# Tokens requested sooner and two memory units run between the steps of the first projection

## The chip, the cores and the metric

The kernel runs on one core of a Trainium2 chip. A core has a matrix engine (TensorE, PE in the profile; its weight loads are PEld), a vector engine (VectorE, DVE), a scalar engine (ScalarE, ACT), GpSimd (POOL) and SyncE (SP), which here issues nearly all DMAs. Each engine works through its own list of instructions in order and waits on semaphores of the others. The metric is the device time of one execution in microseconds (us), the median of several.

## The reference, cut to what matters

```python
mem_n = rmsnorm(mem, norm_mem)                       # 256 memory tokens, width 1024
for i in range(2):                                   # layer 0: mixer A, layer 1: mixer B
    h = rmsnorm(x, norm_mix[i])                      # 1024 tokens, width 1024
    mk, mv = split(mem_n @ w_mem_kv[i])              # 4 memory heads of 64
    q, k, v, qm = split(h @ w_in[i])                 # one combined projection
    y_tok = windowed_gqa(q, k, v, sink) if i == 0 else neighbourhood_attn(q, k, v, rpb)
    y_mem = memory_attn(qm, mk, mv)
    x = x + concat(y_tok, y_mem) @ w_out[i]
    h = rmsnorm(x, norm_ffn[i])
    g, u = split(h @ w_gate_up[i])
    x = x + (silu(g) * u) @ w_down[i]
return rmsnorm(x, norm_final)
```

All arrays are float32. The kernel writes each operand of a product as a high part and a low part (the rest) and multiplies hh, hl and lh, so each 128x128 block of weights costs three products.

## The kernel before, in words

Everything is held transposed: features on the 128 partitions (8 blocks k), tokens along the free dimension in two halves of 512 (index 0 and 1). A "unit" is 128 columns of a weight matrix, 512 KB; `load_w` fetches it, `hi` (L106, a cast on ACT) and `lo` (L109, a subtraction on DVE or POOL) split it. `steps` (L139) multiplies a unit with a half: 8 steps of three matmuls, 24 in all, into one PSUM bank.

The memory stage stands at the start (pool `mp`). It splits the memory tokens (mhl, L301), runs eight memory units (w_mem[l, u], matmuls "mm<-mhl,wm" of 128x256), scales each result (mt, L345), and splits it into keys (mkh, mkl) or transposes it (mvT, L352) into values (mv). In between it prepares the tokens for layer 0. The class Norm squares them (sq on ACT, L196), adds the squares pairwise on DVE (L219), sums over partitions on PE (st, L212), and turns that into a factor: nv on DVE (L232), nr on POOL (L233), a diagonal matrix diag on DVE (L235), spread by one product bc on PE (L247). Then each of the 8 blocks gives h (L267, DVE) and its parts hT (ACT L106, DVE L109). There are three such norms in the stage: the memory's, token half 0's, token half 1's.

`first_dense` ends the stage. It runs three units of the first projection ("wf") on half 0 (72 matmuls of 128x512 "mm<-hT,wf"), and between their steps asks for the squares of half 1 and its norm. It leaves the three results in PSUM, in the list `pre`. It is called again for layer 1, behind the down projection (X, L1327, and the residual adds x, L1291, on DVE). The layer's code then reads `pre` out (`z.put(0, ps)`: copies to QS, KH, vT on ACT, L106, L410 and L464, and the low parts on DVE) and runs the same three units on half 1 (`z.half(1)`, 72 more matmuls). Behind them come memory scores (S, L567), transposes of v (vtr, L427), softmax rows (p) and so on.

PSUM has eight banks in four pools: ps_mm (2), ps_s (2, tag S), ps_t (3, tag T) and ps_o (1, tag O). `mm_tile` counts its calls in `wide[1]`; while `wide[0]` is set, counts 3 and 4 modulo 5 go to an S bank, 0 to a T bank, and 1 and 2 to ps_mm. The layer's code clears `wide[0]`, so half 1 takes ps_mm only. st, mvT and vtr take T banks, bc the O bank; in the down projection X takes ps_mm and S banks, Y the T and O banks.

The text of the kernel sets only dependences and priorities: a scheduler decides the order on each engine when the kernel is built, so the order is shown below as it comes out. Names there carry buffer numbers: mm_791 is the 791st object.

Of the kernel before, what the change touches and what calls it, by code (L numbers as in the profile page):

```python
# [9 lines left out]
F32 = mybir.dt.float32  # L10
F32R = mybir.dt.float32r
AF = mybir.ActivationFunctionType
ALU = mybir.AluOpType
# [4 lines left out]
P = 128  # L18
D = 1024
S = 1024  # L20
NK = D // P
HS = 512
HD = 64
NH = 12
NKV = 4
NMH = 4
# [15 lines left out]
def trunk_kernel(ctx: ExitStack, tc: tile.TileContext, a: dict, out: bass.AP):  # L42
# [58 lines left out]
    def raw_tile(name):  # L101

        return phase[0].tile([P, D], F32, tag="raw", name=name, bufs=phase[2])

    def hi(dst, src):
        nc.scalar.copy(dst, src)  # L106

    def lo(dst, src, h, eng=None):
        (eng or nc.vector).tensor_tensor(dst, src, h.bitcast(F32), op=ALU.subtract)  # L109

    def load_w(src, tag="whl", bufs=3, eng=None, name="w", pool=wp, parts=1):
        raw = raw_tile(f"{name}_raw")
        nc.sync.dma_start(raw, src)
        w = pool.tile([P, 2, D], F32R, tag=tag, name=name, bufs=bufs)
        for i in range(parts):
            c = slice(i * D // parts, (i + 1) * D // parts)
            hi(w[:, 0, c], raw[:, c])
            pieces = 4 if eng is nc.gpsimd else 1
            for j in range(pieces):
                n = D // parts // pieces  # L120
                cj = slice(i * D // parts + j * n, i * D // parts + (j + 1) * n)
                lo(w[:, 1, cj], raw[:, cj], w[:, 0, cj], eng)
        return w
# [9 lines left out]
    def steps(ps, w, h, order=range(NK), n=HS, start=True, stop=True):  # L133

        order = list(order)
        for i, k in enumerate(order):
            terms = three(wk(w, k), (h[k][:, 0, :n], h[k][:, 1, :n]))
            for j, (l, r) in enumerate(terms):
                nc.tensor.matmul(  # L139
                    ps[:, :n], l, r, start=start and i == 0 and j == 0,  # L140
                    stop=stop and i == len(order) - 1 and j == 2,
                )
            yield

    def run(g):
        for _ in g:
            pass

    def run_some(g, n):
        for _ in range(n):  # L150
            next(g, None)

    def first_dense(layer, norm):

        pre = []
        src = a["w_in_a"] if layer == 0 else a["w_in_b"]
        todo = (norm.add(x[k][1]) for k in range(len(norm.xs), NK))
        parts = norm.split(layer, hT[1], 4)
        for n, u in enumerate(FIRST[layer]):
            w = load_w(src[u], eng=None if layer == 0 else nc.gpsimd, name="wf")  # L160
            wide[:] = True, 2 + n
            ps = mm_tile()
            for i, _ in enumerate(steps(ps, w, hT[0])):
                if next(todo, 0) is not None and len(norm.xs) == NK and (n or i > 3):
                    next(parts, None)
            pre.append((w, ps))
        run(parts)
        return pre

    def mm_tile(name="mm"):  # L170

        wide[1] += 1
        if wide[0] and wide[1] % 5 > 2:
            return ps_s.tile([P, HS], F32, tag="S", name=name)
        if wide[0] and wide[1] % 5 == 0:
            return ps_t.tile([P, HS], F32, tag="T", name=name)
        return ps_mm.tile([P, HS], F32, tag="mm", name=name)

    def dense(w, h, n=HS):
        ps = mm_tile()  # L180
        run(steps(ps, w, h, n=n))
        return ps
# [96 lines left out]
    with tc.tile_pool(name="mp", bufs=1, reuse_waits="tile") as mp:  # L279
        phase[:] = mp, 8, 5  # L280
        memt = mp.tile([P, NK, NM], F32, name="memt")
        warm = mp.tile([P, P], F32, name="warm")
        nc.scalar.activation(warm, ones, AF.Square)
        wm0 = raw_tile("wm0")
        nc.sync.dma_start(memt[:, :2], a["mem"][:, :2])
        nc.scalar.dma_start(wm0[:, :HS], a["w_mem"][0, 0][:, :HS])
        nc.sync.dma_start(gains, a["gains"])
        nc.sync.dma_start(memt[:, 2:4], a["mem"][:, 2:4])
        nc.scalar.dma_start(wm0[:, HS:], a["w_mem"][0, 0][:, HS:])
        nc.sync.dma_start(memt[:, 4:], a["mem"][:, 4:])  # L290
        w0 = wp.tile([P, 2, D], F32R, tag="whl", name="wm", bufs=3)
        hi(w0[:, 0, :HS], wm0[:, :HS])
        lo(w0[:, 1, :HS], wm0[:, :HS], w0[:, 0, :HS])
        ws = [w0]


        mh = []
        mhl = mp.tile([P, NK, 2, NM], F32R, name="mhl")
        for k in range(NK):
            t, g = mhl[:, k], gains[:, 4, k : k + 1]  # L300
            nc.scalar.activation(t[:, 0], memt[:, k], AF.Copy, scale=g)  # L301
            nc.vector.scalar_tensor_tensor(
                t[:, 1], memt[:, k], g, t[:, 0].bitcast(F32), op0=ALU.mult, op1=ALU.subtract
            )
            mh.append(t)
            if k == 1:
                hi(w0[:, 0, HS:], wm0[:, HS:])
                lo(w0[:, 1, HS:], wm0[:, HS:], w0[:, 0, HS:])
        ws.append(load_w(a["w_mem"][0, 1], name="wm"))
        nc.sync.dma_start(ident, a["ident"])  # L310

        def load_x(f, k):
            x[k][f] = mp.tile([P, HS], F32, tag=f"x{k}{f}", name=f"x0_{k}{f}")
            nc.sync.dma_start(x[k][f], a["x"][k][:, f * HS : (f + 1) * HS])

        mem_norm = Norm(NM)
        for k in range(NK):
            mem_norm.add(memt[:, k])
        scale = mp.tile([P, NM], F32, name="mscale")
        nc.scalar.copy(scale, mem_norm.scale())  # L320

        hT = [[None] * NK, [None] * NK]
        norms = [Norm(), Norm()]
        kept = []
        for i in range(8):
            l, u = divmod(i, 4)
            if u == 0:
                kh = mp.tile([P, 2, NM], F32R, name=f"mkh{l}", tag="mkh", bufs=2)
                kl = mp.tile([P, 2, NM], F32R, name=f"mkl{l}", tag="mkl", bufs=2)
                vm = mp.tile([P, 2, NMH, 2, HD], F32R, name=f"mv{l}", tag="mv", bufs=2)  # L330
                kept.append((kh, kl, vm))
            if i + 2 < 8:
                ws.append(load_w(a["w_mem"][(i + 2) // 4, (i + 2) % 4], name="wm"))
            if i == 0:
                nc.sync.dma_start(sink, a["sink"].to_broadcast([P, NH]))
                nc.vector.tensor_scalar(nsink, sink, -1.0, None, op0=ALU.mult)
            if i < 3:
                for k in ((0, 1, 2), (3, 4, 5), (6, 7))[i]:
                    load_x(0, k)
            elif i < 7:  # L340
                for k in (2 * i - 6, 2 * i - 5):
                    load_x(1, k)
            ps = dense(ws[i], mh, NM)
            t = temp("mt", NM)
            nc.vector.tensor_tensor(t, ps[:, :NM], scale, op=ALU.mult)  # L345
            if u < 2:
                hi(kh[:, u], t)
                lo(kl[:, u], t, kh[:, u])
            else:
                tr = ps_t.tile([P, HS], F32, tag="T", name="mvT")  # L350
                for b in range(2):
                    nc.tensor.transpose(tr[:, b * P : (b + 1) * P], t[:, b * P : (b + 1) * P], ident)  # L352
                src = tr[:, :NM].rearrange("p (b i d) -> p b i d", b=2, i=2)
                m = 2 * (u - 2)
                for b in range(2):
                    hi(vm[:, b, m : m + 2, 0], src[:, b])
                    lo(vm[:, b, m : m + 2, 1], src[:, b], vm[:, b, m : m + 2, 0])
            if i in (1, 2):
                for k in range(4 * i - 4, 4 * i):
                    norms[0].add(x[k][0])  # L360
            if i == 2:
                parts = norms[0].split(0, hT[0])
            if i > 2:
                run_some(parts, 2)
            if i in (5, 6):
                for k in range(4 * i - 20, 4 * i - 16):
                    norms[1].add(x[k][1])
        pre = first_dense(0, norms[1])
        for l, (kh, kl, vm) in enumerate(kept):
            nc.sync.dma_start(memk_d[l, 0], kh.rearrange("p m k -> p (m k)").bitcast(F32))  # L370
            nc.sync.dma_start(memk_d[l, 1], kl.rearrange("p m k -> p (m k)").bitcast(F32))
            nc.sync.dma_start(memv_d[l], vm.rearrange("p b m i d -> p (b m i d)").bitcast(F32))
# [1158 lines left out]
```

## Time and profile before

| | us |
|---|---|
| runs of before, median (lowest to highest of 3) | 2138.86 (2138.51 to 2140.3) |
| the profiled execution, its own time | 2140.07 |
| its span | 2138.3 |
| PE busy, share of the span | 2099.2, 98% |
| DVE, ACT, POOL busy | 1516.3, 1062.4, 575.6 |
| mean granted clock of PE | 0.995 of full |
| memory stage, from the first matmul to the first memory scores of layer 0 | 5.85 to 86.56 |
| first projection of layer 1, both halves | 1044.16 to 1080.56 |

Rows of the profile name line, engine, operation and "out<-in" tiles. In a timeline the first number is the start in us from the span's start, the second the length of a group of like instructions, "x26" their count, and the bracket the idle time of that engine just before with the instruction that ended it. In windows, PEclk is the clock that was granted to PE, 1.00 being full. The pipelined matmuls of a group overlap, so a group's length divided by its count is the pitch of one.

### The profile page before, as it was taken

The page shows a single profiled execution, that of the slowest core. Times are in us where ns is not written, and L with a number is a line of the kernel's source. Part 1 is how long each engine was busy: PE and PEld are TensorE (multiplying, and loading weights), DVE is VectorE, ACT ScalarE, POOL GpSimd, SP SyncE. Part 2 cuts the span into 40 slices and gives each one's busy share as a digit, 9 for nine tenths or more (in the row PEclk, how much of TensorE's full clock was granted, in tenths as well). Part 3 has the DMA queues.
Part 4 walks back from the last instruction along what each step waited for, and adds up shares of the span by engine and source line. Part 5 has one row for each costly group of instructions (what it writes and reads, how often), then busy time and mean ns, then how long its engine had stood idle before and what let it go on. Part 6 is the DMA issues. An engine that isn't in the chain of part 4 may idle for free.

```text
span 2138.3 us, 29072 instructions
## 1 busy us (share of the span) xinstructions
PE 2099.2 (98%) x10308; PEld 1753.4 (82%) x10308; DVE 1516.3 (71%) x2485; ACT 1062.4 (50%) x2042; POOL 575.6 (27%) x618
## 2 busy tenths in 40 slices
PE   7999999999999999999999999999999999999998
PEld 6788888878888888888778888888888888888887
DVE  7677787798666666867756666677986666677675
ACT  6477775444433434334465666654443434344442
POOL 0344330234443440000223223302243443410000
PEclk9999999999999999999999999999999999999999
DMA  6321018423322336866222212275133323367662
GB/s 249 111 84 50 31 60 285 128 84 120 106 95 104 109 114 241 294 217 211 83 86 81 78 58 67 77 255 179 45 129 114 109 89 107 105 246 261 200 225 88
DMA packets 121170, 287.29 MB, mean 134 GB/s; under 512 B 12352, under 2 KB 20800, under 8 KB 121024
## 3 DMA queue, kind: packets, MB, share of 16 engines
q1 hardware_dynamic: 113712, 272.71, 38.0%
q10 hardware_dynamic: 7312, 12.72, 1.6%
q8 instruction: 82, 1.34, 0.3%
q14 instruction: 64, 0.52, 0.1%
HBM read 210.40 MB, written 68.94 MB: 131 GB/s over the span
## 4 chain that ended last, share of the span: by engine, by line
PE 86%; DVE 5%; ACT 3%; issue 2%; DMA 2%; POOL 1%; SPq 0%; DVEq 0%; ACTq 0%; POOLq 0%
PE X L896 17%; PE Y L896 16%; PE mm L139 14%; PE X L1327 10%; PE po L139 8%; PE Y L1327 7%; PE S L567 3%; PE O L630 3%; PE pT L610 3%; PE X L978 2%; PE Y L978 2%; DVE h L267 1%; DMA wd_raw<-in_w_dn 1%; DVE hT L109 1%; DVE sq L219 0%
## 5 line engine op out<-in xcount | busy, mean ns | idle before, releaser
L896 PE MATMUL Y<-hB,wgu 128*128 128x512 f32 x1056 | 255.5, 391 | 0.8 <-ACT c L916 0.8
L896 PE MATMUL X<-hB,wgu 128*128 128x512 f32 x1056 | 254.8, 391 | 0.0
L1327 PE MATMUL X<-hB,wd 128*128 128x512 f32 (+1 forms) x1092 | 243.8, 383 | 1.1 <-ACT wd L106 1.1
L109 DVE TENSOR_TENSOR wgu<-wS,wgu 128x1024 fp32r<-128x1024 f32 (+1 forms) x124 | 152.9, 1233 | 121.9 <-ACT wgu L106 121.7
L1327 PEld LDWEIGHTS X<-hB,wd 128*128 128x128 f32 x1092 | 200.2, 188 | 42.0 <-ACT wd L106 1.5
L896 PEld LDWEIGHTS Y<-hB,wgu 128*128 128x128 f32 x1056 | 196.7, 188 | 43.4 <-ACT c L916 1.6
L896 PEld LDWEIGHTS X<-hB,wgu 128*128 128x128 f32 x1056 | 195.9, 188 | 39.9
L595 POOL TENSOR_SCALAR p<-p,stat 128x384 f32<-128x384 f32 (+1 forms) x256 | 139.7, 565 | 310.9 <-DVE stat L592 218.7
L139 PE MATMUL mm<-hT,wqk 128*128 128x512 f32 x672 | 195.8, 404 | 1.5 <-DVE KL L109 1.5
L106 ACT CAST wgu<-wS 128x1024 fp32r<-128x1024 f32 (+1 forms) x124 | 114.3, 923 | 149.9 <-POOL wS L853 124.6
L139 PE MATMUL po<-yT,wo 128*128 128x512 f32 x768 | 184.8, 394 | 0.0
L1327 PE MATMUL Y<-hB,wd 128*128 128x512 f32 x792 | 180.7, 389 | 0.3 <-DVE x L1291 0.3
L1327 PEld LDWEIGHTS Y<-hB,wd 128*128 128x128 f32 x792 | 148.5, 188 | 31.8 <-ACT hB L106 0.7
L233 POOL TENSOR_TENSOR nr<-nv,neg_half 128x4 f32<-128x4 f32 (+1 forms) x12 | 12.1, 1009 | 602.1 <-DVE nv L232 602.1
L139 PEld LDWEIGHTS po<-yT,wo 128*128 128x128 f32 x768 | 142.8, 188 | 29.7 <-issue 1.0
L896 PE MATMUL X<-hT,wgu 128*128 128x512 f32 x624 | 150.2, 391 | 0.0
L106 ACT CAST hB<-b_raw 128x512 fp32r<-128x512 f32 x154 | 89.4, 618 | 115.4 <-DMA b_raw<-b_d 94.7
L853 POOL TENSOR_TENSOR wS<-wgu_raw 128x512 f32<-128x512 f32 x44 | 61.0, 1387 | 295.3 <-DVE wgu L109 295.3
L582 ACT ACTIVATE p<-p,stat 128x256 f32<-128x256 f32 (+1 forms) x192 | 112.4, 586 | 52.6 <-DVE stat L578 50.4
L896 PEld LDWEIGHTS X<-hT,wgu 128*128 128x128 f32 x624 | 116.7, 188 | 26.3
L109 DVE TENSOR_TENSOR pl<-pT,ph 128x384 fp32r<-128x384 f32 (+1 forms) x256 | 118.2, 493 | 19.0 <-ACT ph L106 16.1
L896 PE MATMUL Y<-hT,wgu 128*128 128x512 f32 x528 | 129.9, 390 | 0.0
(181 smaller groups left out, 4201.6 us busy)
## 6 DMA issues: line engine op xcount, KB each, us to landing
wgu_raw<-in_w_gu SPq DMA_DIRECT2D x92, 512.0 KB
wd_raw<-in_w_dn SPq DMA_DIRECT2D x70, 512.0 KB
b_raw<-b_d SPq DMA_DIRECT2D x70, 512.0 KB
b_d<-c SPq DMA_DIRECT2D x88, 256.0 KB
b_d<-t SPq DMA_DIRECT2D x66, 256.0 KB
wo_raw<-in_w_out SPq DMA_DIRECT2D x32, 512.0 KB
x<-in_x SPq DMA_DIRECT2D x32, 256.0 KB
xr_d<-x ACTq DMA_DIRECT2D x32, 256.0 KB
```

What stands on the lines that cost most here:

```text
L106: nc.scalar.copy(dst, src)
L109: (eng or nc.vector).tensor_tensor(dst, src, h.bitcast(F32), op=ALU.subtract)
L139: nc.tensor.matmul(ps[:, :n], l, r, start=start and i == 0 and j == 0, stop=stop and i == len(order) - 1 and j == 2,)
L567: nc.tensor.matmul(s_[:, :n], Q[self.h][:, qb * P : (qb + 1) * P], k, start=j == 0, stop=j == 1)
L582: nc.scalar.activation(p[:, :n], p[:, :n], AF.Exp, bias=m1, scale=-1.0, accum_out=s1)
L595: nc.gpsimd.tensor_scalar(p[:, :n], p[:, :n], ri[:, i : i + 1], 1.0, op0=ALU.mult, op1=ALU.mult)
L610: nc.tensor.transpose(tr[:, j * P : (j + 1) * P], p[:, j * P : (j + 1) * P], ident)
L630: nc.tensor.matmul(o[:, c0 : c0 + w * P], self.value(j), t[:, s0 : s0 + w].rearrange("p j q -> p (j q)"), start=j == js[0] and t is self.p ...
L853: sub = lambda o, p_, q_: nc.gpsimd.tensor_tensor(o, p_, q_, op=ALU.subtract)
L896: nc.tensor.matmul(ps, l, r, start=n in (0, 1, 3, 6) and k == 0 and i == 0, stop=k == 3 and i == 2, skip_group_check=True,)
L978: nc.tensor.matmul(bank[:, at : at + h2], l, r, start=start and k == 0 and i == 0, stop=stop and k == 1 and i == 2, skip_group_check=True,)
L1327: nc.tensor.matmul(bank[:, c], l, r, start=i in (0, 1, 3, 6) and p == 0 and n == 0, stop=p == HF - 1 and n == 2, skip_group_check=True,)
```

## The change

It does seven things:

- four products on `ones` run first on PE;
- the tokens come in pairs of blocks (8 DMAs of 512 KB for 16 of 256 KB); those of half 0 are requested ahead of memory units 2 and 3, those of half 1 from the first unit on, and weights four units ahead;
- the memory norm's sums and its factor are asked for later (units 2 and 3);
- a memory product is scaled and split two units later (`finish_wm`);
- units 6 and 7, with weight tiles of their own ("wm8"), run as `more` between the steps of the first wf unit, two steps per step;
- half 1's squares are asked for two at a time, from the first unit's fifth step on (`todo`);
- the counter of `mm_tile` is no longer set in layer 0; in layer 1 it is set to 4 + n instead of 2 + n.

```diff
@@ first_dense
-    def first_dense(layer, norm):
+    def first_dense(layer, norm, more=iter(()), todo=iter(())):
...
-        todo = (norm.add(x[k][1]) for k in range(len(norm.xs), NK))
         parts = norm.split(layer, hT[1], 4)
         for n, u in enumerate(FIRST[layer]):
             w = load_w(src[u], eng=None if layer == 0 else nc.gpsimd, name="wf")
-            wide[:] = True, 2 + n
+            if layer:
+                wide[:] = True, 4 + n
             ps = mm_tile()
             for i, _ in enumerate(steps(ps, w, hT[0])):
-                if next(todo, 0) is not None and len(norm.xs) == NK and (n or i > 3):
-                    next(parts, None)
+                run_some(more, 2)
+                if n or i > 3:
+                    run_some(todo, 2)
+                    if len(norm.xs) == NK:
+                        next(parts, None)
+            run(more)
             pre.append((w, ps))
         run(parts)
@@ memory stage
+        for _ in range(4):
+            nc.tensor.matmul(ps_o.tile([P, HS], F32, tag="O", name="warm")[:, :P], ones, ones, start=True, stop=True)
...
+        load_wm(1)
+        load_x(0, 0)
+        load_x(0, 2)
+        load_wm(2)
+        nc.sync.dma_start(ident, a["ident"])
+        load_x(0, 4)
+        load_x(0, 6)
+        load_wm(3)
...
-            if i + 2 < 8:
-                ws.append(load_w(a["w_mem"][(i + 2) // 4, (i + 2) % 4], name="wm"))
...
-            if i < 3:
-                for k in ((0, 1, 2), (3, 4, 5), (6, 7))[i]:
-                    load_x(0, k)
-            elif i < 7:
-                for k in (2 * i - 6, 2 * i - 5):
-                    load_x(1, k)
-            ps = dense(ws[i], mh, NM)
+            if i + 4 < 8:
+                load_wm(i + 4)
+                load_x(1, 2 * i)
+            if i + 2 < 8:
+                split_wm(i + 2)
             if i in (1, 2):
                 for k in range(4 * i - 4, 4 * i):
                     norms[0].add(x[k][0])
             if i == 2:
-                parts = norms[0].split(0, hT[0])
+                mem_norm.sums()
+            if i < 6:
+                sums[i] = dense(whl[i], mh, NM)
+            if i == 2:
+                parts = norms[0].split(0, hT[0], 1)
+                run_some(parts, 1)
+            if i == 3:
+                nc.scalar.copy(scale, mem_norm.scale())
+                finish_wm(0)
+                finish_wm(1)
+            if 3 < i < 6:
+                finish_wm(i - 2)
             if i > 2:
                 run_some(parts, 2)
-            if i in (5, 6):
-                for k in range(4 * i - 20, 4 * i - 16):
-                    norms[1].add(x[k][1])
-        pre = first_dense(0, norms[1])
+
+        def last_units():
+            for i in (6, 7):
+                finish_wm(i - 2)
+                sums[i] = mm_tile()
+                yield from steps(sums[i], whl[i], mh, n=NM)
+            finish_wm(6)
+            finish_wm(7)
+
+        def tokens():
+            for k in range(NK):
+                norms[1].add(x[k][1])
+                yield
+
+        pre = first_dense(0, norms[1], last_units(), tokens())
```

`finish_wm(i)` holds the lines from `mt` (L345) to the split of mv, `split_wm(i)` a unit's hi and lo, `load_wm` and `load_x` one DMA each.

**PE, layer 0, from the last products of half 0 to the first of half 1.** mm_729 is the bank of the third wf result before and mm_706 after; mm_791 and mm_783 are the first bank of half 1; the brackets name the engines that a row waits for. Before:

```order
L139 MATMUL mm_729<-hT_556,wf_726 128x512 x3
L139 MATMUL mm_729<-hT_561,wf_726 128x512 x3
L139 MATMUL mm_791<-hT_665,wf_612 128x512 [waits Activation_49]
L139 MATMUL mm_791<-hT_665,wf_612 128x512 [waits DVE_49]
L139 MATMUL mm_791<-hT_665,wf_612 128x512
L139 MATMUL mm_791<-hT_673,wf_612 128x512 [waits Activation_49]
L139 MATMUL mm_791<-hT_673,wf_612 128x512 [waits DVE_49]
```

After:

```order
L139 MATMUL mm_649<-hT_501,wf_646 128x512 x3
L139 MATMUL mm_706<-hT_501,wf_703 128x512 x2
L139 MATMUL mm_783<-hT_666,wf_506 128x512 [waits Activation_49]
L139 MATMUL mm_783<-hT_666,wf_506 128x512 [waits DVE_49]
L139 MATMUL mm_783<-hT_666,wf_506 128x512
L139 MATMUL mm_783<-hT_674,wf_506 128x512
L139 MATMUL mm_783<-hT_674,wf_506 128x512 [waits DVE_49]
```

The first product of half 1 waits for ACT in both; the next block's first product waits for ACT before (its own cast) and for nothing of ACT now.

**ACT at the same place**, the last casts of half 1 and the reading of `pre`. mm_615, mm_657, mm_729 are the three results before, mm_509, mm_649, mm_706 after. Before:

```order
L106 CAST hT_721<-h_719 128x512
L106 CAST QS_766<-mm_615 64x16x32
L410 ACTIVATE QS_773<-mm_657 64x512
L464 COPY vT_789<-mm_729 128x16x32
L106 CAST KH_767<-mm_615 64x16x32
L410 ACTIVATE QS_774<-mm_657 64x512
```

After:

```order
L106 CAST hT_728<-h_726 128x512
L106 CAST QS_758<-mm_509 64x16x32
L457 ACTIVATE QS_765<-mm_649 64x512
L511 COPY vT_781<-mm_706 128x16x32
L106 CAST KH_759<-mm_509 64x16x32
L457 ACTIVATE QS_766<-mm_649 64x512
```

The order of ACT is the same; the banks that these rows free are others.

**PE, layer 1, from the end of the down projection (X) on.** mm_9536 and mm_9528 are the first wf result. Before, from the first product, and then around st:

```order
L139 MATMUL mm_9536<-hT_9392,wf_9530 128x512 [waits DVE_49,Activation_49]
...
L212 MATMUL st_9553<-inv_d_108,sq_9349 128x1 [waits DVE_49]
L212 MATMUL st_9553<-inv_d_108,sq_9349 128x1 x3
L139 MATMUL mm_9536<-hT_9466,wf_9530 128x512
L139 MATMUL mm_9581<-hT_9392,wf_9575 128x512 [waits Activation_49]
```

After:

```order
L139 MATMUL mm_9528<-hT_9384,wf_9522 128x512 [waits Activation_49]
...
L139 MATMUL mm_9573<-hT_9389,wf_9567 128x512 x2
L216 MATMUL st_9545<-inv_d_108,sq_9341 128x1 [waits DVE_49]
L216 MATMUL st_9545<-inv_d_108,sq_9341 128x1 x3
L139 MATMUL mm_9573<-hT_9389,wf_9567 128x512
```

The first product no longer waits for DVE, and st has moved from behind 23 products to behind 29. Behind bc stand 43 products of half 0 before and 37 after; half 1 then begins as in layer 0, with one wait for ACT.

More of the change, by code (lines that the diff above doesn't have):

```diff
@@ L283, in trunk_kernel, with load_wm, split_wm, load_x @@
         nc.scalar.activation(warm, ones, AF.Square)
-        wm0 = raw_tile("wm0")
+        for _ in range(4):
+            nc.tensor.matmul(ps_o.tile([P, HS], F32, tag="O", name="warm")[:, :P], ones, ones, start=True, stop=True)
+        def load_wm(i):
+            ws[i] = raw_tile("wm")
+            nc.sync.dma_start(ws[i], a["w_mem"][i // 4, i % 4])
+        def split_wm(i, cs=slice(0, D)):
+            if i not in whl:
+                pool, tag, n = (mp, "wm8", 2) if i > 5 else (wp, "whl", 3)
+                whl[i] = pool.tile([P, 2, D], F32R, tag=tag, name="wm", bufs=n)
+            w = whl[i]
+            hi(w[:, 0, cs], ws[i][:, cs])
+            lo(w[:, 1, cs], ws[i][:, cs], w[:, 0, cs])
+        def load_x(f, k):
+            t = mp.tile([P, 2, HS], F32, tag=f"x{k}{f}", name=f"x0_{k}{f}")
+            nc.sync.dma_start(
+                t, a["x"][k : k + 2].rearrange("m p t -> p m t")[:, :, f * HS : (f + 1) * HS]
+            )
+            x[k][f], x[k + 1][f] = t[:, 0], t[:, 1]
+        ws, whl = {}, {}
+        ws[0] = raw_tile("wm0")
         nc.sync.dma_start(memt[:, :2], a["mem"][:, :2])
-        nc.scalar.dma_start(wm0[:, :HS], a["w_mem"][0, 0][:, :HS])
+        nc.scalar.dma_start(ws[0][:, :HS], a["w_mem"][0, 0][:, :HS])
         nc.sync.dma_start(gains, a["gains"])
         nc.sync.dma_start(memt[:, 2:4], a["mem"][:, 2:4])
-        nc.scalar.dma_start(wm0[:, HS:], a["w_mem"][0, 0][:, HS:])
+        nc.scalar.dma_start(ws[0][:, HS:], a["w_mem"][0, 0][:, HS:])
         nc.sync.dma_start(memt[:, 4:], a["mem"][:, 4:])
[L291 to L294, printed above, removed]
+        load_wm(1)
[6 more added lines that the diff above has]
+        load_wm(3)
+        nc.sync.dma_start(sink, a["sink"].to_broadcast([P, NH]))
+        split_wm(0, cs=slice(0, HS))
         mh = []
         mhl = mp.tile([P, NK, 2, NM], F32R, name="mhl")
+        mem_norm = Norm(NM)
         for k in range(NK):
@@ L306, in trunk_kernel, with finish_wm @@
             if k == 1:
[L307 to L316, printed above, removed]
+                split_wm(0, cs=slice(HS, D))
+        split_wm(1)
         for k in range(NK):
             mem_norm.add(memt[:, k])
-        scale = mp.tile([P, NM], F32, name="mscale")
-        nc.scalar.copy(scale, mem_norm.scale())
+        nc.vector.tensor_scalar(nsink, sink, -1.0, None, op0=ALU.mult)
         hT = [[None] * NK, [None] * NK]
         norms = [Norm(), Norm()]
[L324 to L331, printed above, removed]
-            if i + 2 < 8:
-                ws.append(load_w(a["w_mem"][(i + 2) // 4, (i + 2) % 4], name="wm"))
-            if i == 0:
-                nc.sync.dma_start(sink, a["sink"].to_broadcast([P, NH]))
-                nc.vector.tensor_scalar(nsink, sink, -1.0, None, op0=ALU.mult)
-            if i < 3:
-                for k in ((0, 1, 2), (3, 4, 5), (6, 7))[i]:
-                    load_x(0, k)
-            elif i < 7:
-                for k in (2 * i - 6, 2 * i - 5):
-                    load_x(1, k)
-            ps = dense(ws[i], mh, NM)
+        scale = mp.tile([P, NM], F32, name="mscale")
+        kept, sums = [], {}
+        def finish_wm(i):
+            (kh, kl, vm), u, ps = kept[i // 4], i % 4, sums.pop(i)
             t = temp("mt", NM)
@@ L348, in trunk_kernel @@
                 lo(kl[:, u], t, kh[:, u])
[L349 to L357, printed above, removed]
+                return
+            tr = ps_t.tile([P, HS], F32, tag="T", name="mvT")
+            for b in range(2):
+                nc.tensor.transpose(tr[:, b * P : (b + 1) * P], t[:, b * P : (b + 1) * P], ident)
+            src = tr[:, :NM].rearrange("p (b i d) -> p b i d", b=2, i=2)
+            m = 2 * (u - 2)
+            for b in range(2):
+                hi(vm[:, b, m : m + 2, 0], src[:, b])
+                lo(vm[:, b, m : m + 2, 1], src[:, b], vm[:, b, m : m + 2, 0])
+        parts = iter(())
+        for i in range(8):
+            if i % 4 == 0:
+                l = i // 4
+                kh = mp.tile([P, 2, NM], F32R, name=f"mkh{l}", tag="mkh", bufs=2)
+                kl = mp.tile([P, 2, NM], F32R, name=f"mkl{l}", tag="mkl", bufs=2)
+                vm = mp.tile([P, 2, NMH, 2, HD], F32R, name=f"mv{l}", tag="mv", bufs=2)
+                kept.append((kh, kl, vm))
+            if i + 4 < 8:
[3 more added lines that the diff above has]
+                split_wm(i + 2)
             if i in (1, 2):
```

## The prediction

> **What bounds the kernel now.** I read the page first (busy shares, chain), then the stage that the change touches by windows and timelines, then the second place at which the edited helper is used.
>
> ```profile
> PE 2099.2 (98%) x10308; PEld 1753.4 (82%) x10308; DVE 1516.3 (71%) x2485; ACT 1062.4 (50%) x2042; POOL 575.6 (27%) x618
> PE 86%; DVE 5%; ACT 3%; issue 2%; DMA 2%; POOL 1%; SPq 0%; DVEq 0%; ACTq 0%; POOLq 0%
> ```
>
> TensorE (PE) is busy 98% of the span and is 86% of the chain, so only idle time of PE, and time at the half clock, can be won or lost. The memory stage is where it is not full. In the windows below the columns are start:end, length, busy time of PE, PEld, DVE, ACT and POOL, PE's granted clock, DMA share, GB/s; the second row, of PE alone, has PE's busy time, clock, DMA share and GB/s.
>
> ```profile
> 16.00:61.90 45.90, 38.75 (x212) 32.58 (x212) 36.14 (x65) 23.80 (x45) 3.58 (x3) 0.85 0.54 199
> 23.00:26.50 3.50, 0.32 (x3) 1.00 1.03 392
> ```
>
> From 16 to 61.9 us PE stands for 7.2 us and has a mean clock of 0.85; VectorE (DVE) works 36.14 of 45.9 us. At 23 us the loads run at 392 GB/s and PE has nothing to do. The timeline of PE (start, length, count, in brackets idle time and who ended it):
>
> ```profile
> 5.85 6.05 PE L139 MATMUL mm<-mhl,wm 128*128 128x256 f32 x26 [5.85 <-ACT mhl L301]
> 26.41 0.74 PE L139 MATMUL mm<-mhl,wm 128*128 128x256 f32 x2 [3.18 <-ACT wm L106]
> 35.14 1.82 PE L247 MATMUL bc<-diag,ones 128*128 128x512 f32 x2
> 47.71 2.57 PE L139 MATMUL mm<-hT,wf 128*128 128x512 f32 x10 [1.42 <-DVE wf L109]
> 55.65 0.44 PE L352 MATMUL mvT<-ident,mt 128*128 128x128 f32 x2 [1.41 <-DVE mt L345]
> 56.40 0.95 PE L212 MATMUL st<-inv_d,sq 128*128 128x1 f32 x8
> 61.87 1.02 PE L247 MATMUL bc<-diag,ones 128*128 128x512 f32 x2
> 62.33 24.40 PE L139 MATMUL mm<-hT,wf 128*128 128x512 f32 x105
> 86.56 0.28 PE L567 MATMUL S<-mKH,QS 128*128 128x256 f32 x1
> ```
>
> The bc at 61.87 is the norm of token half 1. Behind it PE has 105 products and no gap until 86.56: 33 left of half 0, then 72 of half 1, which start as soon as the first hT of half 1 is there. So before, the end of this stage is bc + 24.7 us.
>
> **The change, part by part.** *Loads and warm products.* The sixteen token requests on SyncE's queue become eight of twice the size, with the same bytes; those of half 0 pass w_mem units 2 to 4, which come 1, 1.25 and 0.5 MB later (at 392 GB/s 2.7, 3.3 and 1.3 us). The 3.18 us wait at 26.41 ended with a memory weight, so these loads matter; in the new order that time is filled with products whose weights are split already, and DVE becomes what PE waits for. The four products on ones lie in the 5.85 us in which PE waits for the first mhl: nothing, between 0 and, if they should bring the full clock sooner, a gain below 1 us. The private tiles of units 6 and 7 and the transfers of the finished keys hide behind DVE.
>
> *The third bc.* I lay the new order of each engine out with the durations of these rows (form and count, busy time, mean ns of one):
>
> ```profile
> L219 DVE TENSOR_TENSOR sq<-sq 128x512 f32<-128x512 f32 x14 | 9.1, 685 | 0.3 <-ACT sq L196 0.3
> L109 DVE TENSOR_TENSOR hT<-h,hT 128x512 fp32r<-128x512 f32 x8 | 5.4, 686 | 0.0
> L109 DVE TENSOR_TENSOR wf<-wf_raw,wf 128x1024 fp32r<-128x1024 f32 x3 | 3.7, 1218 | 0.0
> L345 DVE TENSOR_TENSOR mt<-mm,mscale 128x256 f32<-128x256 f32 x8 | 3.3, 419 | 0.1
> L109 DVE TENSOR_TENSOR mv<-mvT,mv 128x128 fp32r<-128x128 f32 x8 | 2.3, 285 | 0.4 <-ACT mv L106 0.4
> L109 DVE TENSOR_TENSOR mkl<-mt,mkh 128x256 fp32r<-128x256 f32 x4 | 1.6, 422 | 0.1
> L235 DVE TENSOR_TENSOR diag<-ident,nr 128x512 f32<-128x512 f32 x2 | 1.4, 693 | 1.8 <-POOL nr L233 1.8
> ```
>
> DVE's work from 16 us to the lo part of the first wf is that 36.14 us less what now stands behind it: 7 sq, 2 wf, 4 mt, 4 mv, 2 mkl, 1 hT, 1 diag, by the means 12.3 us, less 0.08 us of overlap each (the means of the whole window sum to 41.6 us against 36.14 busy), so 10.5. That leaves 25.6 us, with some 1.8 us of waits for the first norms: the lo part is ready at 43.5. Unit 7's weights are split some 6 us of DVE rows earlier; behind that stand two products of wf, a transpose and its own 24, so PE is through with the memory units by about 41 and waits 2.5 to 3 us. 38 products of wf at 0.232 us (24.40/105) bring it to 52.4, where st stands; DVE has then merged the squares as well (1 hT, 2 mt, 2 mkl, 2 wf and 7 sq behind the first wf, 8.5 us: 52.0). If the wait halves the clock for one window, st is at 54.1. From st to bc it is 3.64 us in layer 1 (49.86 to 53.50, rows below). So bc comes at 56.0 or 57.7; I take 57.2, nearer to the halved clock: 4.7 us earlier than 61.87. By itself that is a gain.
>
> *The banks.* What `pre` holds has moved. mm_tile counts: before, the counter was set to 2, 3, 4 and the three half-0 results lay in two S banks and a T bank, so both ps_mm banks were free for half 1, which takes only those. Now the counter runs on in layer 0 (7, 10, 11: mm, T, mm) and is set to 4, 5, 6 in layer 1 (T, mm, mm). Both ps_mm banks hold results, and the first product of half 1 waits until one is read out. In the order it waits once for ScalarE (ACT) and its followers no more, where before each k waited for its own cast: the count it waits for lies behind all eight hT casts. ACT frees a bank with the vT copy:
>
> ```profile
> 71.27 1.28 ACT L106 CAST hT<-h 128x512 fp32r<-128x512 f32 x2 [1.84 <-DVE h L267]
> 73.43 0.57 ACT L464 COPY vT<-mm 128x512 f32<-128x512 f32 x1
> ```
>
> It ends at 74.00, 12.13 us after bc; the DVE rows that feed the casts are the same now. So half 1 starts at 57.2 + 12.13 + 0.1 = 69.4 and needs 72 x 0.232 = 16.7 us: 86.1. PE has finished its 28 products of half 0 at about 64.2 and stands for 5.2 us, and all 72 products and the first S behind them with it; the only ones that wait for these are ACT's later copies. What that does to the clock, this trace shows:
>
> ```profile
> 53.80:57.20 3.40, 1.99 (x14) 1.00 0.00 0
> 57.20:60.60 3.40, 3.40 (x10) 0.50 0.24 96
> 1101.70:1105.10 3.40, 1.85 (x11) 1.00 0.41 122
> 1105.20:1108.60 3.40, 3.40 (x17) 1.00 0.69 177
> ```
>
> A window of 3.41 us with 1.99 us of PE work (st and transposes among it) was followed by one at half clock; one with 1.85 us of fuller products was not. A wait of 5.2 us leaves one window with less than either, so at least one halved window of work: 1.7 us, at most about 2.6. I take 2.1. Layer 0's stage ends at 88.2 against 86.56: +1.7 us. With bc at 56.0 it would be +0.5, at 57.7 and 2.6 of clock +2.7.
>
> *Layer 1* uses the same helper, with rows of its own (PE, then DVE and ACT):
>
> ```profile
> 1039.84 3.56 PE L1327 MATMUL X<-hB,wd 128*128 128x512 f32 x15
> 1044.16 5.50 PE L139 MATMUL mm<-hT,wf 128*128 128x512 f32 x23 [0.76 <-DVE x L1291]
> 1049.86 1.05 PE L212 MATMUL st<-inv_d,sq 128*128 128x1 f32 x8 [0.20 <-DVE sq L219]
> 1053.50 1.12 PE L247 MATMUL bc<-diag,ones 128*128 128x512 f32 x2 [1.09 <-DVE diag L235]
> 1054.06 26.66 PE L139 MATMUL mm<-hT,wf 128*128 128x512 f32 x115
> 1080.56 0.60 PE L427 MATMUL vtr<-ident,vT 128*128 128x128 f32 x4
> ...
> 1045.68 4.12 DVE L219 TENSOR_TENSOR sq<-sq 128x512 f32<-128x512 f32 x4
> ...
> 1065.16 0.57 ACT L464 COPY vT<-mm 128x512 f32<-128x512 f32 x1
> ```
>
> The first wf tile took an S bank that the down projection's X had just left, hence 0.76 us of waiting for DVE's x; in a T bank that goes, and PE starts at 1043.4. But 29 products now stand ahead of st, not 23: st at 1043.4 + 29 x 0.232 = 1050.1 (DVE's sq, done at 1049.8, is no longer late), bc at 1053.8, vT read out at 1053.8 + 12.2 = 1066.0. 37 products behind bc end at 1062.9, so PE stands for 3.2 us; then 16.7 us: 1082.8 against 1080.56, +2.2. The 3.2 us fall on one or two windows; only where they split into two parts below 2 us is there a chance that the clock holds, so I add 1.4 of at most 1.7 (below: none). Layer 1: +3.6, between +2.2 and +3.9.
>
> *Behind it.* In layer 0 ACT and POOL split the next weights during the wait instead of between the softmax steps; one wait that this could take away:
>
> ```profile
> 98.71 0.44 PE L610 MATMUL pT<-ident,p 128*128 128x128 f32 x2 [0.95 <-POOL p L595]
> ```
>
> Against it, a weight cast (1.05 us) now stands ahead of the first softmax rows on ACT, and the third S tile waits for its bank for about 0.5 us. I take -0.4, between -1 and +0.5.
>
> **Sum:** +1.7 + 3.6 - 0.4 = +4.9 us on the profiled execution (2140.07 us, span 2138.3); that execution is 1.2 us above the median of the runs, 2138.86, so for the median 2143.8 us, +0.23%. With all lower ends +1.7 (2140.6), with all upper +7.1 (2146.0).
>
> **Rivals.** *No wait for a bank* (the other side): if a ps_mm bank is released by a reader ahead of the hT casts, half 1 starts right behind half 0. Then layer 0 ends at 57.2 + 24.7 = 81.9, -4.7, and layer 1 keeps its 0.76: -5.4, 2133.5 us, faster. Against it speaks ACT's row order, where all readers of the three results stand behind the eighth cast. It decides where the vT copy lies: layer 0 breaks even with half 1 starting at 67.8 or so, 10.6 us behind bc instead of 12.2.
>
> *The clock holds behind layer 1's wait:* 3.6 becomes 2.2, and the time 2142.4, within 0.2%. For it speaks the undisturbed window at 1101.7 us, against it the halved one at 57.2.
> The Trainium skill, page "TensorE: Matmul & The Clock Gate", section "Part 1: The HAM clock gate", says that half rate follows a whole idle window of about 3.4 us, and its table on why this matters warns of gaps beyond some 3 us. By that rule 3.2 us would not be enough and the sum would be this rival's. The trace disagrees in part: a window with 1.99 us of work was enough at 57.2 us.
>
> *The third bc doesn't come sooner:* DVE is nearly full from 16 to 52 us, and PE's small waits there may halve the clock as they did for 10 us before. Each microsecond that bc comes later is one lost; with bc at 60 the time is 2146.6, slower.
>
> **How the numbers follow.** 0.2% of the time, 4.3 us, is about what a measurement tells from no change: faster is below 2134.6, slower above 2143.1. The forecast has 0.52; its own range, 2141 to 2146, holds the upper bound, and I put 0.36 of it above and 0.16 within. The held clock has 0.20 (0.17 within, 0.03 above), the late bc 0.13 (above), no wait 0.12 (0.10 faster, 0.02 within), the rest 0.03 (within). Together: faster 0.10, same 0.38, slower 0.52. The range reaches from 2137, between no wait and the lower ends, to 2147.5, just over the late bc.
>
> **What would show it.** In the new profile: the third bc at 56 to 58 us; a gap of about 5 us on PE ended by ACT's vT copy at 69 to 70, a halved window behind it, the first S of layer 0 at 87 to 89; near 1043 no wait for x, and one of about 3 us ended by vT at 1066 (plus what layer 0 adds). The prediction is wrong if one of these gaps is missing, or if the stages behind give back more than 1 us.

## The result, and the profile after

| | before | changed |
|---|---|---|
| median of 22 runs each, us | 2138.82 (2136.78 to 2140.61) | 2143.02 (2140.3 to 2146.12) |
| ratio, 95% interval | | 1.002 [1.0013, 1.0026] |
| profiled execution, us (span) | 2140.07 (2138.3) | 2146.12 (2144.3) |

The changed kernel is 0.2% slower: 4.2 us, where 4.9 were forecast (2143.8 us). The profiled execution of the changed kernel is the longest of its 22, so its places are read here and its sum is not.

PE does the same work, with the four products on `ones` added, in a longer span:

```profile
PE 2100.7 (98%) x10316; PEld 1754.5 (82%) x10316; DVE 1515.7 (71%) x2485; ACT 1060.9 (49%) x2042; POOL 575.6 (27%) x618
```

The timeline of PE in the memory stage, the rows that answer to those of before (line numbers are 47 higher in most of the code and 4 higher in the helpers):

```profile
26.50 1.12 PE L251 MATMUL bc<-diag,ones 128*128 128x512 f32 x2 [0.75 <-DVE diag L239]
44.11 10.54 PE L139 MATMUL mm<-hT,wf 128*128 128x512 f32 x38 [2.77 <-DVE wf L109]
54.49 0.95 PE L216 MATMUL st<-inv_d,sq 128*128 128x1 f32 x8
57.57 1.13 PE L251 MATMUL bc<-diag,ones 128*128 128x512 f32 x2 [0.64 <-DVE diag L239]
58.89 6.17 PE L139 MATMUL mm<-hT,wf 128*128 128x512 f32 x26
70.04 18.96 PE L139 MATMUL mm<-hT,wf 128*128 128x512 f32 x72 [4.98 <-ACT vT L511]
88.84 0.28 PE L614 MATMUL S<-mKH,QS 128*128 128x256 f32 x1
```

The norm of half 1 is spread at 57.57 us instead of 61.87, and the stage nevertheless ends at 88.84 instead of 86.56. In between stands the new gap: 4.98 us, ended by ACT's copy of vT, and behind it 72 products that take 18.96 us. ACT's row, and the windows of the clock around the gap (PE busy, clock, DMA share, GB/s):

```profile
69.42 0.57 ACT L511 COPY vT<-mm 128x512 f32<-128x512 f32 x1
64.86:68.27 3.41, 0.19 (x1) 1.00 0.97 246
68.27:71.68 3.41, 1.64 (x4) 0.50 0.69 220
71.68:75.10 3.42, 3.42 (x10) 0.50 0.64 253
```

The copy ends at 69.99 and the first product of half 1 starts at 70.04. Two windows at half clock follow, the first of them partly idle. In layer 1 the same gap comes back, shorter:

```profile
1039.82 4.92 PE L1374 MATMUL X<-hB,wd 128*128 128x512 f32 x21
1044.58 6.74 PE L139 MATMUL mm<-hT,wf 128*128 128x512 f32 x29
1051.23 1.05 PE L216 MATMUL st<-inv_d,sq 128*128 128x1 f32 x8
1054.86 1.13 PE L251 MATMUL bc<-diag,ones 128*128 128x512 f32 x2 [1.08 <-DVE diag L239]
1055.42 8.97 PE L139 MATMUL mm<-hT,wf 128*128 128x512 f32 x37
1067.14 18.24 PE L139 MATMUL mm<-hT,wf 128*128 128x512 f32 x72 [2.74 <-ACT vT L511]
1085.22 0.60 PE L474 MATMUL vtr<-ident,vT 128*128 128x128 f32 x4
```

No wait for x stands in front of the first wf product any more, and st comes behind 29 products. From the last X product to the first vtr it takes 40.5 us instead of 37.2.

### The profile page after: what moved, and what is told of

Same layout as the page of the kernel before. It is cut to its first block, busy times and chain, and to the rows that moved or that the text cites. A ratio compares the mean times of both kernels' runs of the same rounds, so it can differ in the third digit from the quotient of the medians.

```text
span 2144.3 us, 29083 instructions
## 1 busy us (share of the span) xinstructions
PE 2100.7 (98%) x10316; PEld 1754.5 (82%) x10316; DVE 1515.7 (71%) x2485; ACT 1060.9 (49%) x2042; POOL 575.6 (27%) x618
## 4 chain that ended last, share of the span: by engine, by line
PE 86%; DVE 6%; ACT 3%; DMA 3%; issue 1%; POOL 1%; SPq 0%; DVEq 0%; POOLq 0%; ACTq 0%
PE X L943 16%; PE Y L943 16%; PE mm L139 15%; PE X L1374 11%; PE po L139 8%; PE Y L1374 6%; PE S L614 3%; PE O L677 3%; PE pT L657 3%; PE X L1025 2%; PE Y L1025 2%; DMA wd_raw<-in_w_dn 1%; DMA b_raw<-b_d 1%; DVE h L271 1%; DVE wgu L109 1%
## 5 line engine op out<-in xcount | busy, mean ns | idle before, releaser
L109 DVE TENSOR_TENSOR hB<-b_raw,hB 128x512 fp32r<-128x512 f32 x154 | 99.8, 688 | 44.7 <-ACT hB L106 44.6
```

## The experiments

Each run had runs of the kernel before beside it on the same chip; differences of 2 us are about what the intervals of 10 or 11 runs resolve, so the places in the traces carry the finer readings.

### Layer 0's banks as before

```diff
-            if layer:
-                wide[:] = True, 4 + n
+            wide[:] = True, (4 if layer else 2) + n
...
                 finish_wm(i - 2)
+                wide[1] = i - 6
                 sums[i] = mm_tile()
```

> The changed kernel with layer 0's three results in S, S and T banks as before (units 6 and 7 of the memory stage take ps_mm); layer 1 as changed. Theory (the wait for a bank costs 5 us and two halved clock windows): half 1 of layer 0 starts right behind half 0, at about 67 us instead of 70, without a halved window behind it; first memory scores at 84 instead of 88.8 us; 4 to 5 us less than the changed kernel, about 2138.5 us. Rival (the late start comes from the norm, not from the banks): half 1 starts at 69 to 70 us anyway and the time stays within 1 us of the changed kernel.

Measured: 2140.27 us, ratio to before 1.0009 [1.0, 1.0018]. PE's timeline:

```profile
59.20 1.02 PE L250 MATMUL bc<-diag,ones 128*128 128x512 f32 x2
59.65 25.09 PE L139 MATMUL mm<-hT,wf 128*128 128x512 f32 x108
84.58 0.28 PE L614 MATMUL S<-mKH,QS 128*128 128x256 f32 x1
```

All 36 + 72 products behind bc run without a gap, though bc itself is 1.6 us later: st starts where it does in the changed kernel (54.52 against 54.49), but 10 products of half 0 stand between it and bc instead of 6. Half 1 starts at 68.26, while ACT's copy of vT ends only at 71.33. The first scores come at 84.58, 4.3 us sooner than in the changed kernel. The rival falls: the norm did not hold half 1 up, the bank did. The medians show 2.7 us of it, less than the 4 to 5 expected.

### Layer 1's banks as before

```diff
             if layer:
-                wide[:] = True, 4 + n
+                wide[:] = True, 2 + n
```

> The changed kernel with layer 1's three results in S, S and T banks as before; layer 0 as changed. Theory: the 2.7 us gap at 1067 us and the halved window behind it go, the 0.76 us wait for x at 1043 comes back; the stretch from the last X product to the first vtr is 37.2 us as before instead of 40.6; 3.5 us less than the changed kernel, about 2139.5 us. Rival (layer 1's gap is given back in the attention behind it): less than 1 us.

Measured: 2139.09 us, 1.0002 [0.9993, 1.0011]. From the last X product to the first vtr it takes 37.15 us again, with the 0.76 us wait for x back. So the time is that of before with everything of the change left in layer 0. The interval reaches from -1.5 to +2.4 us: a cost of the new memory stage with its gap of 5 us isn't seen over the whole kernel, but the +1.3 us that the prediction had for it aren't excluded.

### No result in ps_mm, in either layer

```diff
-            if layer:
-                wide[:] = True, 4 + n
+            wide[:] = True, (4, 2, 3)[n] if layer else 2 + n
...
+                wide[1] = i - 6
                 sums[i] = mm_tile()
```

> The changed kernel with layer 0's results in S, S, T and layer 1's in T, S, S banks: no result in ps_mm, and the first one of layer 1 in a bank that X never used. Theory: both gains and neither wait, 4.5 us less than the kernel before, 2134.3 us (between 2133 and 2136). Rival (some of the sooner norm is lost behind the stage, since the attention of layer 0 is not bound by PE alone): 2137 to 2139.

Measured: 2134.93 us, 0.9984 [0.9975, 0.9993]: within the theory's 2133 to 2136 us, 3.4 us less than before by the ratio and 8 us less than the changed kernel. In layer 1:

```profile
1038.99 6.73 PE L139 MATMUL mm<-hT,wf 128*128 128x512 f32 x29
1049.83 25.32 PE L139 MATMUL mm<-hT,wf 128*128 128x512 f32 x109
1074.99 0.60 PE L474 MATMUL vtr<-ident,vT 128*128 128x128 f32 x4
```

The first wf product starts without a wait, half 1 follows half 0 without a gap, and from X's end to vtr it takes 35.8 us, 1.3 less than before.

### The waits filled with products

```diff
         run(parts)
+        f = ps_t.tile([P, HS], F32, tag="T", name="fill")
+        for j in range(10 if layer else 18):
+            nc.tensor.matmul(f, pre[0][0][:, 0, :P], hT[0][j % NK][:, 0], start=True, stop=True)
         return pre
```

> The changed kernel with 18 (layer 0) and 10 (layer 1) products without use in a free T bank behind the last products of half 0, so that PE works through most of both waits. Theory (the clock is halved because of the gaps): half 1 starts when it did, its 72 products take 16.7 us in both layers instead of 18.96 and 18.24; 3 to 4 us less than the changed kernel, about 2139.5 us. Rival (the clock halves for another reason, or the gap of 2.7 us in layer 1 was not what halved it): only layer 0 gains, 2.3 us, about 2140.7 us, or nothing.

Measured: 2140.1 us, 1.0006 [0.9997, 1.0015]. Half 1 of layer 0 and of layer 1:

```profile
70.08 16.64 PE L139 MATMUL mm<-hT,wf 128*128 128x512 f32 x72 [0.90 <-ACT vT L514]
1063.77 16.64 PE L139 MATMUL mm<-hT,wf 128*128 128x512 f32 x72 [0.48 <-ACT vT L514]
```

Half 1 starts where it did (70.08 against 70.04), and its 72 products take 16.64 us in both layers instead of 18.96 and 18.24. So 2.3 and 1.6 us of the loss are the clock that was halved behind the gaps, not the gaps themselves. The medians show 2.9 us of them.

### Without the four products on ones

```diff
-        for _ in range(4):
-            nc.tensor.matmul(ps_o.tile([P, HS], F32, tag="O", name="warm")[:, :P], ones, ones, start=True, stop=True)
```

> The changed kernel without the four products on ones at the start. Theory (they lie in time in which PE waits for the first mhl, and do not change the granted clock): first product at 6.0 us, third bc at 56.5 to 57.7 us, time as the changed kernel, 2143 us. Rival (they bring the full clock sooner): third bc 0.5 to 1 us later, up to 1 us slower.

Measured: 2144.54 us, 1.0023 [1.0013, 1.0032], beside the changed kernel's 1.002: the same within the intervals. The first product comes at 5.60 us, the third bc at 58.11, 0.4 us above the expected bracket and 0.5 us later than in the changed kernel, which is what the rival expected. There is one more halved window here (at 24 to 27 us) than in the first profile of the changed kernel; but a second execution of that kernel, with the products on `ones`, has a halved window at the same place (23.6 to 27.0). A gain below 1 us from these products is neither shown nor excluded.

### Weights ahead of the tokens

```diff
         load_wm(1)
-        load_x(0, 0)
-        load_x(0, 2)
-        load_wm(2)
         nc.sync.dma_start(ident, a["ident"])
-        load_x(0, 4)
-        load_x(0, 6)
-        load_wm(3)
+        load_wm(2)
         nc.sync.dma_start(sink, a["sink"].to_broadcast([P, NH]))
+        load_x(0, 0)
+        load_wm(3)
+        load_x(0, 2)
+        load_x(0, 4)
+        load_wm(4)
+        load_x(0, 6)
```

> The changed kernel with the weights of units 1 to 4 requested ahead of most tokens, nearly in the order of before (still in pairs). Theory A (the sooner tokens move the norm of half 1): the norm of half 0 has its bc 2 to 4 us later than 26.5 us, and the third bc comes 2 to 3 us later than 57.6, so 2 to 3 us slower than the changed kernel. Theory B (DVE is full from 16 to 52 us, so that the order of loads matters only for when its work can begin): the second bc is 1 to 2 us later, the third within 1 us, the time within 1 us.

Measured: 2144.14 us, 1.0022 [1.0013, 1.0031]. The bc of half 0 and of half 1:

```profile
27.58 1.78 PE L251 MATMUL bc<-diag,ones 128*128 128x512 f32 x2
58.05 1.12 PE L251 MATMUL bc<-diag,ones 128*128 128x512 f32 x2 [0.64 <-DVE diag L239]
```

Theory B: 1.1 us later and 0.5 us later than in the changed kernel, and the time is the same within the intervals. A second execution of the changed kernel has its bc of half 0 at 27.61, so even the 1.1 us need not come from the order. The order of the requests, which gives the change its name, is worth less than these measurements resolve (some 2 us).

### Units 6 and 7 ahead of the first projection

```diff
-            if i < 6:
-                sums[i] = dense(whl[i], mh, NM)
+            sums[i] = dense(whl[i], mh, NM)
...
                 finish_wm(i - 2)
-                sums[i] = mm_tile()
-                yield from steps(sums[i], whl[i], mh, n=NM)
+                yield
```

> The changed kernel with units 6 and 7 run ahead of the first projection as before, their results read out where the changed kernel does. The count of mm_tile then gives S, T and one ps_mm bank to layer 0's results, so that half 1 finds a free bank; layer 1 as changed. It is to be compared with the run that has layer 0's banks restored (2140.3 us, first scores at 84.6). Theory (the interleaving fills little, since PE waits for DVE there): third bc within 1.5 us of that run's 59.2, time within 1.5 us of it. Rival (the interleaving is what makes the norm come sooner): third bc at 61 us or later, 2 us or more slower.

Measured: 2142.32 us, 1.0012 [1.0003, 1.0021]. PE's wait ahead of st, and the bc:

```profile
55.24 0.80 PE L139 MATMUL mm<-hT,wf 128*128 128x512 f32 x1 [3.24 <-DVE wf L109]
62.42 1.02 PE L251 MATMUL bc<-diag,ones 128*128 128x512 f32 x2
```

The places fit the rival: the third bc comes 3.2 us later than in the run with layer 0's banks restored (58.81 in the run without a result in ps_mm, which has the same order there), and the first scores at 87.09 instead of 84.58. Without the two units in between, PE waits twice for split weights, 3.02 us for the first wf and 3.24 for the second, where the other run waits once, 5.16 us; and three windows are halved ahead of bc instead of two (here the clock is half from 55 to 62 us). The time does not show it: the ratio is 1.0012 against the other run's 1.0009. So what the interleaving is worth rests on single executions.

### Before, with layer 1's banks of the change

```diff
-            wide[:] = True, 2 + n
+            wide[:] = True, (4 if layer else 2) + n
```

> The kernel before with one number changed: layer 1's three results in T, mm and mm banks, as in the changed kernel. Theory: the gap of 2.7 us and one halved window at layer 1's half 1 as in the changed kernel, less 0.76 us in front: 3.5 us slower than before, 2142.3 us. Rival (the gap is given back behind, or needs the rest of the change): within 1.5 us of before.

Measured: 2140.22 us, 1.0005 [0.9996, 1.0014]; 11 runs between 2137.95 and 2143.31. The gap is there, but no halved window follows it in this execution (timeline, and three windows of PE around it):

```profile
1063.17 16.62 PE L139 MATMUL mm<-hT,wf 128*128 128x512 f32 x72 [2.76 <-ACT vT L464]
1058.01:1061.43 3.42, 2.40 (x11) 1.00 0.72 282
1061.43:1064.84 3.41, 1.67 (x7) 1.00 0.00 0
1064.84:1068.25 3.41, 3.41 (x16) 1.00 0.02 5
```

The same windows of the changed kernel's first profile:

```profile
1061.54:1064.95 3.41, 2.86 (x13) 1.00 0.87 341
1064.95:1068.37 3.42, 1.23 (x5) 1.00 0.03 7
1068.37:1071.79 3.42, 3.42 (x9) 0.50 0.00 0
```

In one the boundary of the windows cuts the gap into 1.02 and 1.74 us, in the other into 0.55 and 2.19. From X's end to vtr it takes 38.85 us here: +1.7 on before's 37.16, not the expected 3.5. The expectation was right on the gap and counted the halved window as certain. The median, 1.1 us above before's, lies in the rival's bracket, but the gap is not given back in this stretch.

### Both kernels once more

> The kernel before once more, for its clock. Theory: how many windows of 3.41 us run at half clock in the memory stage differs between executions, and the third bc with it: 58.8 us with two halved windows (as in the run before this one with only layer 1's banks changed), 61.9 us with four; here within 58.5 to 62 us. Rival (the third bc at 61.9 us belongs to this kernel in every execution): 61.5 to 62.2 us.

> The changed kernel once more, for its clock. Theory: the gap of about 2.75 us in layer 1 halves the clock where one window of 3.41 us holds 1.9 us of it or more, so its 72 products take 18.2 us then and 16.6 us otherwise; layer 0's gap of 5 us always does. Rival (the gap halves the clock always in this kernel): 18.2 us.

One execution each, 2139.83 and 2141.36 us. The third bc of before, and that of the run above, which has the same memory stage:

```profile
61.29 1.02 PE L247 MATMUL bc<-diag,ones 128*128 128x512 f32 x2
58.84 1.13 PE L247 MATMUL bc<-diag,ones 128*128 128x512 f32 x2
```

It lies at 58.84, 61.29 and 61.87 in three executions, with two, four and four halved windows ahead of it. The 61.29 alone would not have settled it, 0.2 us below the rival's bracket; the 58.84, with the same order on PE, does. The changed memory stage has its third bc at 57.57, 57.00, 57.61 and 56.57 (the two executions of the changed kernel, and the runs with the waits filled and with layer 1's banks as before). So the change gains between 1.2 and 5.3 us there, 3.5 by the means. In the changed kernel's second execution layer 1's gap was cut into 0.94 and 1.78 us, and the clock held, as the theory expected:

```profile
1066.46 16.62 PE L139 MATMUL mm<-hT,wf 128*128 128x512 f32 x72 [2.72 <-ACT vT L511]
```

Over the seven profiles with this gap (2.72 to 2.76 us): a window followed at half clock where one window held 1.98 us of the gap or more (the changed kernel's first execution, and the runs with layer 0's banks, weights first and units ahead), and none where the larger part was 1.78 or less (without the four products on `ones`, before with the new banks, the changed kernel's second execution).

## Why the prediction was right

**The banks** (shown). Both new gaps stand where the prediction put them, ended by ACT's vT: 4.98 us for 5.2 forecast, 2.74 for 3.2. Taking the banks back removed each one by itself, and both together made the kernel faster than before. The rival without a wait is what the run with no result in ps_mm shows: it has 2134.93 us, and that rival's sum was 2133.5. The two are near each other partly by luck: in that run's profile layer 0's stage ends 2.4 us sooner than before, not 4.7, and layer 1 (1.3 us) and the stretch up to po (1.9 us, below) give the rest.

**The third bc** came at 57.57 (57.2 forecast), and at 57.00 in the second execution. The step's way there held: PE waits 2.77 us for the low part of the first wf, made by DVE, one window behind it is halved, and st comes at 54.49 (54.1 forecast); from st to bc it took 3.08 us instead of 3.64, so that two small errors offset each other. That DVE places it also fits the run with the weights first, where it moved by only 0.5 us. The rival of a later bc did not occur in the changed kernel. What the step took from one execution is the value of before: ahead of 61.87 lie four halved windows, ahead of 58.84 in another execution two.

**The clock behind layer 0's gap**: 18.96 - 16.64 = 2.3 us for 2.1 forecast. The vT copy ended 12.42 us behind bc for 12.13, and the stage ended 2.28 us later for 1.7.

**Layer 1**: +3.3 us in the first profile for 3.6 forecast (40.48 against 37.16), but +1.7 in the second execution. The term mixed a fixed part with one that depends on the execution: the halved window falls in some and not in others, so the rival of the held clock was not another world but part of this one's spread: three of the seven executions with this gap were so.

The Trainium skill, page "TensorE: Matmul & The Clock Gate", section "Part 1: The HAM clock gate", has free-running windows of 3.4 us and half rate after an idle one. The traces agree on windows that do not start with the kernel's work: in the two executions of the changed kernel the same gap was cut into 0.55 and 2.19 us and into 0.94 and 1.78. They differ on idle: windows with 1.23 and, ahead of 57 us in the kernel before, 1.99 us of work were followed by half clock, so 3.4 us of idle time are not needed; the gap of 2.74 us, shorter than the 3.2 that by this rule would not be enough, was followed by it in four of seven executions.

**Behind it** is the step that failed, in size and in its cause: -0.4 forecast, -2.5 measured. The prediction had named as a sign of being wrong that the stages behind give back more than 1 us; up to po they do. From the first scores to the first product of the output projection (po), in the kernel before and then the changed one:

```profile
294.72 0.93 PE L139 MATMUL po<-yT,wo 128*128 128x512 f32 x3
294.51 0.95 PE L139 MATMUL po<-yT,wo 128*128 128x512 f32 x3
```

The changed kernel reaches the first scores 2.3 us later and po 0.2 us sooner: 205.7 us against 208.2. PE's busy time from 84 to 340 us and its waits for softmax rows there say where it comes from; before first, then changed:

```profile
84.00:340.00 256.00, 249.95 (x1405) 1.00 0.24 76
PE pT L610 <- DVE pl L109: 2.9, 6, 0.9
PE pT L610 <- POOL p L595: 1.8, 4, 0.9
...
84.00:340.00 256.00, 251.76 (x1418) 1.00 0.24 75
PE pT L657 <- DVE pl L109: 1.4, 4, 0.5
PE pT L657 <- POOL p L642: 1.4, 4, 0.5
```

(The last three numbers of a wait are its sum in us, how often, and the longest.) 1.9 us of waits are gone. The prediction named one of these, of 0.95 us, and set a new wait for an S bank against it. Its cause was that ACT and POOL split the next weights during PE's wait for the bank. The runs in which layer 0 has no such wait speak against that: po in the runs with layer 0's banks as before and without a result in ps_mm (first scores at 84.58 and 84.18):

```profile
290.89 0.94 PE L139 MATMUL po<-yT,wo 128*128 128x512 f32 x3
290.47 0.95 PE L139 MATMUL po<-yT,wo 128*128 128x512 f32 x3
```

That is 206.3 us from the first scores to po in both, and 206.1 in the run with units 6 and 7 ahead, against 208.0 to 208.4 in three executions of the memory stage of before and 205.7 in the changed kernel. So about 2 of the 2.5 us come without any wait for a bank, and at most some 0.6 us can be put down to it. Which part of the new memory stage gives the 2 us stays open; it is still there with the weights ahead of the tokens (206.2 us) and without the products on `ones` (206.0).

The terms together: in the first profiles layer 0's stage +2.3, behind it -2.5, layer 1 +3.3. That makes 3.1 us, where the medians differ by 4.2 [2.8, 5.6] and these two spans by 6.0. The means of two executions of each kernel place more of it:

| stretch | changed - before, us |
|---|---|
| up to the first scores of layer 0 | +2.4 |
| from there to po | -2.6 |
| from po to the last X product of layer 0 | +1.3 |
| from there to the first vtr of layer 1 | +2.5 |
| from there to the end | +0.3 |
| together | +3.8 |

The third row is a stretch for which the prediction named nothing. Nothing here shows that it belongs to the change: three runs that share the changed kernel's order in layer 0 or nearly so (layer 1's banks as before, without the products on `ones`, weights first) need 748.4 to 748.7 us there, as the kernel before (748.7 and 749.0), and only the two executions of the changed kernel itself 750.0 and 750.2. So the direction and the two gaps were foreseen for the right reason. That the total came out within 1 us of the forecast is in part luck: 2 us more were given back than forecast, layer 1 lost about 1 us less, and a longer stage of layer 0 and a stretch without a term made up for most of it.

## What to carry to other kernels

When results are parked in PSUM across a stage, look where the next stage takes its banks: a parked result in that pool ties the first product to the last reader's place in its engine's order, and everything gained ahead of it is waited away. A gap on PE costs its length and, if one window of the clock gets most of it, the half clock behind it (here 1.6 us behind a gap of 2.74 us, 2.3 behind one of 4.98); a few useless products in the gap show how much is which. Read places that depend on the clock from several executions: here one norm's bc moved by 3 us between executions with the same order on PE.

## What the runs showed of the hardware

The clock of PE is set in windows of 3.41 us that run through the whole execution: in the changed kernel's first profile it is half from 68.27 to 75.10 and from 1068.37 to 1071.79, stretches of two windows and of one, and the 1000.10 us between their starts are 293 windows of 3.413 us. A gap of 2.75 us does or doesn't halve it by how a window boundary cuts it: at 1.98 us or more of idle time in one window it did in four executions, at 1.78 or less in three it did not. These bounds hold for this gap between products of 128x512. In the memory stage a window with less idle time was followed by half clock too: in the run without a result in ps_mm the one from 20.44 to 23.85, with 2.65 us of work, eight products of 128x1 among it.

Behind the gap of layer 0 (4.95 to 4.99 us), a window at half clock with 1.09 to 1.99 us of work was followed by another in four executions; one with 2.83 us of work (weights first) was followed by full clock.
